# Conv taps in a new order and of another kind, and later transposes of q and k, in a transformer block kernel

## The chip, the cores and the metric

One core of one Trainium2 chip runs the whole kernel. The metric is device time in microseconds (us) for one execution; lower is better. Several runs are made, and their median is given.

## The reference, cut to what matters

The function is one block with two feed-forward parts and a mixer between them, in fp32, for 256 positions and a width of 2048. The change touches the mixer alone, and in it the convolution and the preparation of q and k:

```python
proj = h @ w_in                      # 256 x 2048 times 2048 x 5120
q, k, v, conv_a, conv_g = split(proj)
q = apply_rope(rms_norm(q, q_norm)); k = apply_rope(rms_norm(k, k_norm))   # 16 heads of 64
attn = diff_attention(q, k, v, lam)  # causal softmax of two score maps, their difference times v
u = conv_a * sigmoid(conv_g)         # 1024 channels
u = causal_depthwise_conv(u, conv_w, conv_b)   # 31 taps a channel
u = silu(layer_norm(u))
y = concat(rms_norm(attn), u) @ w_out
```

A depthwise convolution of 31 taps is, per channel, a sum of 31 copies of u, each moved by d = 30 - j positions and multiplied by the channel's weight for tap j.

## The kernel before, in words

Activations stand with the contraction dimension on the partitions, so a weight tile of 512 rows by 512 columns is multiplied in 4 row blocks for 2 position tiles, and each product is made of three matmuls (high times high, high times low, low times high: `mm3`, lines 317 to 319) of an fp32 value split in two fp32r parts. One weight tile is thus 24 matmuls of 512 columns. A weight tile comes by one DMA from SP's queue into `raw`. ScalarE makes the high part of each half of it (`whi`, line 296), VectorE subtracts to get the low part (`wlo`, line 298). `whi` and `wlo` have four buffers each, so four half tiles.

The mixer's projection is a loop over 10 column chunks `ci` of `w_in` (line 1045), each of 4 weight tiles `pc` (3 in the loop for the first three chunks, whose first tiles are done ahead of it). Chunks 0 to 3 are convolution channels, two channel tiles of 128 each (so the convolution's 8 channel tiles are done in two halves of four: half 0 from chunks 0 and 1, half 1 from chunks 2 and 3); chunks 4 to 7 are q, k, q, k (`qk_chunk`, two groups of 4 head pairs), chunks 8 and 9 are v. A chunk's accumulators stay in PSUM until its work is done behind the first tile of the next chunk (`finish_mix`).

Side work is cut into pieces and issued between tiles, in the program's order:

- `later` (lines 159 to 172): functions that are to run n weight tiles later. `tick`, called at the end of every tile's matmuls, counts all entries down and runs from the head of the list while the head's count is at zero or below; an entry behind one that is not due waits for it. The transposes of q and k (line 859) stand here with n = 1, one entry for each of two position tiles; the entry that hands a k group's 8 attention score units to `probs` stands behind them.
- `bg` (lines 147 to 153): convolution taps with a cost in units. `fill(n)` takes from the head until n units are used. `TAPS[ci]` is the n of each tile of chunk ci, `TAPS_OUT` that of the first two tiles of the output projection, after which all is drained and the layer norm of the convolution starts (`conv_ln`).

There are two kinds of tap. A plain tap (`conv_tap`, lines 762 to 773) is one VectorE instruction on one channel tile (multiply and add, line 773), or for j = 30 one ScalarE instruction with the bias (line 771). A wide tap (`conv_wide`, lines 775 to 783) does four channel tiles: four ScalarE multiplies into a block `pr` (line 781) and one VectorE add of 4 x 256 elements (line 783). Before, 8 taps of each half are wide (j = 22 to 29). They are queued when the half's second chunk is done, as one run of 8 at 3 units each, ahead of that chunk's plain taps, behind what is left of the first chunk's.

VectorE's work on a q or k chunk (lines 844 to 855, for each position tile): a scalar step of the root mean square (line 143), which follows ScalarE's eight squares (line 843), then a product with a cosine table (848), two with a sine table (853) and their sum (855). The result `A` comes from `tmp`, a pool of six buffers. After it, four transposes on TensorE (line 830) and copies by ScalarE (833, 835, 836).

The order of instructions on each engine is laid out when the kernel is built, by a list scheduler that follows the program's order and lets an instruction that is ready pass one that waits. On the chip each engine runs its list in that order.

Of the kernel before, what the change touches and what calls it, by code (L numbers as in the profile page):

```python
# [24 lines left out]
P = 128  # L25
D = 2048
S = 256
NT = 2
# [5 lines left out]
DH = 64  # L34
CK = 31
# [12 lines left out]
DUE = ((19, 8), (55, 16), (107, 24), (150, 32))  # L48


TAPS = (6, 5, 6, 6, 6, 6, 8, 6, 6, 6)
TAPS_OUT = 12
WIDE = tuple(range(CK - 9, CK - 1))
RMS_EPS = 1e-6
LN_EPS = 1e-5
LAM_INIT = 0.8 - 0.6 * float(np.exp(-0.3 * 0))
# [20 lines left out]
def block_kernel(ctx: ExitStack, tc: tile.TileContext, x_in, pos_in, w_ada, small, w_gu1, w_dn1,  # L77
# [15 lines left out]
    def nm(s):  # L93
        uid[0] += 1
        return f"{s}_{uid[0]}"

    def blk(shape, dtype=F32):
        return blkp.tile(shape, dtype, tag="blk", name=nm("blk"))

    def tmp(shape, dtype=F32):  # L100
        return tmpp.tile(shape, dtype, tag="tmp", name=nm("tmp"))

    def sm(shape, tag="sm"):
        return smp.tile(shape, F32, tag=tag, name=nm(tag))

    def acc_tile(shape=(P, 512)):
        return accp.tile(list(shape), F32, tag="acc", name=nm("acc"))

    def tp_tile(shape=(P, 512)):
        return tpp.tile(list(shape), F32, tag="tp", name=nm("tp"))  # L110
# [23 lines left out]
    for i in range(4):  # L134
        pc = acc_tile()
# [5 lines left out]
    def rstd_of(ss, n, count, eps):  # L141

        nc.vector.tensor_scalar(out=ss, in0=ss, scalar1=1.0 / count, scalar2=eps, op0=ALU.mult, op1=ALU.add)
        nc.gpsimd.tensor_tensor(out=ss, in0=ss, in1=half[:, :n], op=ALU.pow)


    bg = deque()

    def fill(n):
        while n > 0 and bg:  # L150
            units, fn = bg.popleft()
            fn()
            n -= units
# [7 lines left out]
    def after_tiles(n, fn):  # L161
        later.append([n, fn])
# [44 lines left out]
    def ada_share(r, limit):  # L207
        credit[0] += r
        while credit[0] >= 1.0:
            credit[0] -= 1.0  # L210
            if ada_next[0] < limit:
                ada(ada_next[0])
                ada_next[0] += 1
# [113 lines left out]
    def mm_tile(accs, w, act, k0, start, stop, ts=(0, 1), ks=(0, 4)):  # L327

        for j in range(*ks):
            for t in ts:  # L330
                last_mm[0] = mm3(accs[t], act(k0 + j, t), w(j), start and j == ks[0], stop and j == ks[1] - 1)
        tick()
# [14 lines left out]
    class Norm:  # L347
# [28 lines left out]
        def transposed(self, xn):  # L376
            tp = tp_tile((P, 4, P))
            for j in range(4):
                nc.tensor.transpose(tp[:, j, :], xn[:, j * P:(j + 1) * P], ident)  # L379
            return tp, tmp([P, 4, P])  # L380
# [381 lines left out]
    def conv_tap(cc, i, j):  # L762
        ct = 2 * cc + i
        y = ytile[ct // 4][:, ct % 4, :]
        p0 = _COLS["convw"][0] + ct * CK + j
        w = cst[:, p0:p0 + 1]
        d = CK - 1 - j
        u = uT[cc][:, i, :S - d]
        if d == 0:
            b0 = _COLS["convb"][0] + ct  # L770
            nc.scalar.activation(out=y, in_=u, func=AF.Identity, scale=w, bias=cst[:, b0:b0 + 1])  # L771
        else:
            nc.vector.scalar_tensor_tensor(out=y[:, d:], in0=u, scalar=w, in1=y[:, d:], op0=ALU.mult, op1=ALU.add)  # L773

    def conv_wide(b, j):

        d = CK - 1 - j
        pr = blk([P, 4, S])
        for i in range(4):
            p0 = _COLS["convw"][0] + (4 * b + i) * CK + j  # L780
            nc.scalar.activation(out=pr[:, i, d:], in_=uT[2 * b + i // 2][:, i % 2, :S - d], func=AF.Identity,  # L781
                                 scale=cst[:, p0:p0 + 1])
        nc.vector.tensor_add(out=ytile[b][:, :, d:], in0=pr[:, :, d:], in1=ytile[b][:, :, d:])

    def conv_chunk(cc, accs):
        us = []
        for t in range(NT):
            sg = tmp([P, 256])
            nc.scalar.activation(out=sg, in_=accs[t][:, 256:], func=AF.Sigmoid)
            u = tmp([P, 256])  # L790
            nc.vector.tensor_mul(out=u, in0=accs[t][:, :256], in1=sg)
            us.append(u)

        def rest():
            tp = tp_tile((P, 2, S))
            for t in range(NT):
                for i in range(2):
                    nc.tensor.transpose(tp[:, i, t * P:(t + 1) * P], us[t][:, i * P:(i + 1) * P], ident)
            uT[cc] = blk([P, 2, S])
            nc.scalar.copy(out=uT[cc], in_=tp)  # L800
            if cc % 2:
                for i in range(2):
                    bg.append((0, lambda i=i: conv_tap(cc, i, CK - 1)))
                for j in WIDE:
                    bg.append((3, lambda j=j: conv_wide(cc // 2, j)))
            for j in reversed(range(CK)):
                for i in range(2):
                    if j not in WIDE and not (cc % 2 and j == CK - 1):
                        bg.append((1, lambda i=i, j=j: conv_tap(cc, i, j)))

        after_tiles(1, rest)

# [2 lines left out]
    def qk_chunk(name, g, accs):  # L815
        gc, gs = gcs["qn" if name == "q" else "kn"]
        if name == "q":
            dst = blk([P, 4, S])
            qT[g] = dst
        else:  # L820
            dst = [blk([P, 4, S]) for _ in range(2)]
            nc.gpsimd.memset(dst[0][DH:, :, :], 0.0)
            nc.gpsimd.memset(dst[1][:DH, :, :], 0.0)
            kz[g] = dst

        def transposed(t, A):
            tp = tp_tile((P, 4, P))
            Af = A.rearrange("p h d -> p (h d)")
            for i in range(4):
                nc.tensor.transpose(tp[:, i, :], Af[:, i * P:(i + 1) * P], ident)  # L830
            ts = slice(t * P, (t + 1) * P)
            if name == "q":
                nc.scalar.copy(out=dst[:, :, ts], in_=tp)
            else:
                nc.scalar.copy(out=dst[0][:DH, :, ts], in_=tp[:DH])
                nc.scalar.copy(out=dst[1][DH:, :, ts], in_=tp[DH:])

        for t in range(NT):
            a3 = accs[t].rearrange("p (h d) -> p h d", d=DH)
            sq = tmp([P, 8, DH])  # L840
            rs = sm([P, 8], "rs8")
            for i in range(8):
                nc.scalar.activation(out=sq[:, i, :], in_=a3[:, i, :], func=AF.Square, accum_out=rs[:, i:i + 1])  # L843
            rstd_of(rs, 8, DH, RMS_EPS)
            if name == "q":
                rq_of[g, t] = rs
            A = tmp([P, 8, DH])
            nc.vector.tensor_mul(out=A, in0=a3, in1=gc[:, t, :].unsqueeze(1).to_broadcast([P, 8, DH]))
            B = tmp([P, 8, DH])
            for h2 in range(2):  # L850
                o = slice(32 * h2, 32 * h2 + 32)
                r = slice(32 - 32 * h2, 64 - 32 * h2)
                nc.vector.tensor_mul(out=B[:, :, o], in0=a3[:, :, r],
                                     in1=gs[:, t, o].unsqueeze(1).to_broadcast([P, 8, 32]))
            nc.vector.tensor_add(out=A, in0=A, in1=B)
            if name == "k":
                for i in range(8):
                    nc.scalar.activation(out=A[:, i, :], in_=A[:, i, :], func=AF.Identity, scale=rs[:, i:i + 1])  # L858
            after_tiles(1, lambda t=t, A=A: transposed(t, A))

    def v_chunk(g, accs):
        v = blk([P, NT, 512])
# [182 lines left out]
    for ci in range(10):  # L1045
        p0 = 1 if ci < HOLD else 0
        accs = first[ci][2] if ci < HOLD else [acc_tile() for _ in range(NT)]
        for pc in range(p0, 4):
            if ci == 0 and pc < 3:
                for t in range(NT):  # L1050
                    st.piece(pc + 1, t)
            w = w_tile(w_in[ci, pc], ci == 0 and pc <= PRE)
            if ci == 1 or ci == 0 and pc > 1:
                ada_share(1.0, 104)
            mm_tile(accs, w, act, 4 * pc, pc == 0, pc == 3)
            if pc == p0:
                while pend:
                    finish_mix(*pend.pop(0))
            if pc == 3 and ci < 4:
                conv_chunk(ci, accs)  # L1060
            fill(TAPS[ci])
            for _ in range(UNITS):
                if probs:
                    attn_probs(*probs.popleft())
                if avq:
                    attn_av(*avq.popleft())
        if ci >= 4:
            pend.append((ci, accs))
# [136 lines left out]
```

## Time and profile before

| what | value |
|---|---|
| median of 3 runs | 1851.36 us (1848.5 to 1851.45) |
| the profiled execution's own time | 1849.3 us |
| its span in the profile | 1847.5 us |
| TensorE matmul busy (PE) | 1820.4 us, 99% of the span |
| TensorE weight load busy (PEld) | 1501.3 us, 81% |
| VectorE busy (DVE) | 1436.7 us, 78% |
| ScalarE busy (ACT) | 935.3 us, 51% |
| granted TensorE clock, mean | 0.996 |

Busy shares are means over stages; the projection of the mixer stands at about 770 to 1012 us of the span, its output projection from there to about 1103 us. Instructions overlap at their ends: two that follow each other without a gap start closer together than one lasts, so what an instruction takes of a full engine is read from the distance of starts, and its listed length is a little more.

### The profile page before, as it was taken

The numbers are of one execution on the slowest core, as the hardware profiler recorded it, in microseconds if no ns is written. First come the engines' busy times: TensorE is split into PE (matmuls) and PEld (weight loads), VectorE is DVE, ScalarE is ACT, GpSimd is POOL, SyncE is SP. The second block draws the span as 40 slices with busy tenths as digits, with TensorE's granted clock in tenths as the row PEclk, the third lists the DMA queues.
The fourth block names the chain that finished last, engine by engine and source line by source line (L and its number), as shares of the span: only waits on it lengthen the run. The fifth ranks groups of instructions, "written<-read, shape, count | busy, mean of one in ns | idle before, by whom it ended". The sixth has DMA issues, their size and how long they took to land.

```text
span 1847.5 us, 21913 instructions
## 1 busy us (share of the span) xinstructions
PE 1820.4 (99%) x8247; PEld 1501.3 (81%) x8247; DVE 1436.7 (78%) x1874; ACT 935.3 (51%) x1442; POOL 30.2 (2%) x29
## 2 busy tenths in 40 slices
PE   6999999999999999999999999999999999999999
PEld 5788888888888887888888788888888888888887
DVE  7789969998888777898998768878877765544443
ACT  6554444444444433567798655664444444433332
POOL 0000000000000000000111000000000000000000
PEclk8999999999999999999999999999999999999999
DMA  9888968889889898765444557988777755565552
GB/s 382 348 314 309 337 256 316 336 307 339 322 332 365 335 357 329 283 251 182 171 150 159 177 210 305 334 335 317 274 279 273 275 191 195 183 211 211 199 211 80
DMA packets 72729, 495.91 MB, mean 268 GB/s; under 512 B 8192, under 2 KB 8624, under 8 KB 15152
## 3 DMA queue, kind: packets, MB, share of 16 engines
q1 hardware_dynamic: 72624, 494.53, 72.0%
q8 instruction: 64, 1.05, 0.2%
q14 instruction: 41, 0.34, 0.0%
HBM read 492.37 MB, written 2.12 MB: 268 GB/s over the span
## 4 chain that ended last, share of the span: by engine, by line
PE 90%; DVE 5%; ACT 2%; DMA 2%; issue 1%; POOL 0%; SPq 0%; POOLq 0%; DVEq 0%; ACTq 0%
PE acc L318 29%; PE acc L319 29%; PE acc L317 29%; DVE wlo L298 2%; DVE blk L773 1%; DMA raw<-in_w_ada_dram 1%; PE tp L590 1%; ACT whi L296 1%; PE acc L881 1%; ACT blk L781 1%; PE tp L379 1%; DMA blk<-in_w_ada_dram 1%; DVE raw L183 0%; ACT tmp L858 0%; ACT tmp L843 0%
## 5 line engine op out<-in xcount | busy, mean ns | idle before, releaser
L296 ACT CAST whi<-raw 128x1024 fp32r<-128x1024 f32 (+1 forms) x605 | 628.1, 1047 | 719.6 <-PE acc L319 589.2
L298 DVE TENSOR_TENSOR wlo<-raw,whi 128x1024 fp32r<-128x1024 f32 (+1 forms) x605 | 725.6, 1214 | 318.4 <-ACT whi L296 317.0
L317 PE MATMUL acc<-whi,blk 128*128 128x512 f32 x2448 | 955.7, 393 | 5.8 <-ACT blk L388 2.2
L318 PE MATMUL acc<-wlo,blk 128*128 128x512 f32 x2448 | 956.1, 391 | 3.9 <-DVE wlo L298 3.8
L319 PE MATMUL acc<-whi,blk 128*128 128x512 f32 x2448 | 955.2, 390 | 0.0
L317 PEld LDWEIGHTS acc<-whi,blk 128*128 128x128 f32 x2448 | 460.2, 188 | 102.2 <-ACT whi L296 2.8
L318 PEld LDWEIGHTS acc<-wlo,blk 128*128 128x128 f32 x2448 | 460.4, 188 | 100.9 <-DVE wlo L298 7.6
L319 PEld LDWEIGHTS acc<-whi,blk 128*128 128x128 f32 x2448 | 460.1, 188 | 96.8 <-DVE blk L390 0.9
L183 DVE CUSTOM_DVE_ANT_0 raw<-raw,c_bc 128x2048 f32<-128x2048 f32 x142 | 324.5, 2287 | 7.1 <-DMA raw<-in_w_ada_dram 7.0
L470 ACT COPY blk<-acc 128x512 f32<-128x512 f32 x88 | 50.0, 590 | 60.0 <-PE acc L319 58.0
L773 DVE SCALAR_TENSOR_TENSOR blk<-blk,cst,blk 128x245 f32<-128x245 f32 (+21 forms) x176 | 70.8, 468 | 0.6 <-ACT blk L771 0.5
L582 DVE TENSOR_TENSOR blk<-acc,blk 128x512 f32<-128x512 f32 x88 | 57.0, 684 | 0.3
L319 PE MATMUL acc<-blk,blk 128*128 128x512 f32 x112 | 43.7, 392 | 0.0
L317 PE MATMUL acc<-blk,blk 128*128 128x512 f32 x112 | 43.7, 393 | 0.0
L318 PE MATMUL acc<-blk,blk 128*128 128x512 f32 x112 | 43.7, 390 | 0.0
L298 DVE TENSOR_TENSOR blk<-raw,blk 128x1024 fp32r<-128x1024 f32 x28 | 33.8, 1222 | 1.6 <-ACT blk L296 1.6
L584 DVE TENSOR_TENSOR blk<-blk 128x256 f32<-128x256 f32 x88 | 33.5, 420 | 0.7 <-ACT blk L583 0.7
L583 ACT ACTIVATE blk<-blk 128x256 f32<-128x256 f32 x88 | 32.3, 412 | 1.2 <-DVE blk L582 1.1
L296 ACT CAST blk<-raw 128x1024 fp32r<-128x1024 f32 x28 | 28.8, 1050 | 7.0 <-DMA raw<-in_w_dn_dram 5.9
L336 DVE TENSOR_TENSOR blk<-tp,blk 128x512 fp32r<-128x512 f32 x44 | 30.0, 685 | 2.2 <-ACT blk L335 2.2
L345 ACT ACTIVATE tmp<-xall 128x512 f32<-128x512 f32 x22 | 13.8, 632 | 30.3 <-DVE xall L643 17.0
L590 PEld LDWEIGHTS tp<-cst,blk 128*128 128x128 f32 x176 | 21.6, 140 | 6.6 <-DVE blk L336 1.4
(151 smaller groups left out, 717.3 us busy)
## 6 DMA issues: line engine op xcount, KB each, us to landing
raw<-in_w_gu_dram SPq DMA_DIRECT2D x161, 1024.0 KB, 5.4
raw<-in_w_ada_dram SPq DMA_DIRECT2D x142, 1024.0 KB, 6.1
raw<-in_w_dn_dram SPq DMA_DIRECT2D x88, 1024.0 KB, 4.8
raw<-in_w_in_dram SPq DMA_DIRECT2D x40, 1024.0 KB, 4.8
raw<-in_w_out_dram SPq DMA_DIRECT2D x16, 1024.0 KB, 4.8
raw<-in_w_gu_dram SPq DMA_DIRECT2D x8, 768.0 KB, 5.4
blk<-in_w_gu_dram SPq DMA_DIRECT2D x10, 512.0 KB, 13.9
blk<-gate_line SPq DMA_DIRECT2D x6, 512.0 KB, 6.3
```

The costliest lines, as they stand in the source:

```text
L183: nc.vector.tensor_tensor_reduce(out=raw, in0=raw, in1=c_bc, scale=1.0, scalar=0.0, op0=ALU.mult, op1=ALU.add, accum_out=ada_cols[g][:, j ...
L296: nc.scalar.copy(out=hi[:, :m, :], in_=rw)
L298: nc.vector.tensor_sub(out=lo[:, :m, :], in0=rw, in1=hi[:, :m, :].bitcast(F32))
L317: nc.tensor.matmul(acc, ah, wh, start=start, stop=False)
L318: nc.tensor.matmul(acc, ah, wl, start=False, stop=False)
L319: return nc.tensor.matmul(acc, al, wh, start=False, stop=stop)
L470: last_part[0] = nc.scalar.copy(out=parts[c][:, t, :], in_=accs[t])
L582: nc.vector.tensor_add(out=p[:, t, :], in0=accs[t], in1=p[:, t, :])
L583: nc.scalar.activation(out=p[:, t, :256], in_=p[:, t, :256], func=AF.Silu)
L584: nc.vector.tensor_mul(out=p[:, t, 256:], in0=p[:, t, :256], in1=p[:, t, 256:])
L590: nc.tensor.transpose(tp[:, i, t * P:(t + 1) * P], p[:, t, 256 + i * P:256 + (i + 1) * P], ident)
L773: nc.vector.scalar_tensor_tensor(out=y[:, d:], in0=u, scalar=w, in1=y[:, d:], op0=ALU.mult, op1=ALU.add)
```

## The change

The wide taps of half 0 become twelve (j = 18 to 29), those of half 1 stay eight. In the second chunk of a half they no longer come as one run: the plain taps are queued in order, and a wide tap is put in behind every third of them, at 2.6 units. The two ScalarE taps (j = 30) of that chunk cost a unit each as in the first. `TAPS` gets two numbers for each chunk: one for its first tile in the loop, behind which the previous q, k or v chunk is finished, and one for the others. The transposes of q and k go into `later` with n = 2, and `A` is a slice of one block for both position tiles, from the pool of 28 blocks in place of `tmp`.

```diff
-TAPS = (6, 5, 6, 6, 6, 6, 8, 6, 6, 6)
+TAPS = ((6, 6), (5, 5), (6, 6), (6, 7), (7, 7), (2, 7), (2, 7), (2, 7), (2, 7), (4, 7))
 TAPS_OUT = 12
-WIDE = tuple(range(CK - 9, CK - 1))
+
+WIDE = (tuple(range(CK - 13, CK - 1)), tuple(range(CK - 9, CK - 1)))
@@ conv_chunk
-            if cc % 2:
-                for i in range(2):
-                    bg.append((0, lambda i=i: conv_tap(cc, i, CK - 1)))
-                for j in WIDE:
-                    bg.append((3, lambda j=j: conv_wide(cc // 2, j)))
-            for j in reversed(range(CK)):
-                for i in range(2):
-                    if j not in WIDE and not (cc % 2 and j == CK - 1):
-                        bg.append((1, lambda i=i, j=j: conv_tap(cc, i, j)))
+            wide = WIDE[cc // 2]
+            plain = [(i, j) for j in reversed(range(CK)) for i in range(2) if j not in wide]
+            for n, (i, j) in enumerate(plain):
+                bg.append((1, lambda i=i, j=j: conv_tap(cc, i, j)))
+                if cc % 2 and n % 3 == 1 and n // 3 < len(wide):
+                    bg.append((2.6, lambda j=wide[n // 3]: conv_wide(cc // 2, j)))
@@ qk_chunk
+        both = blk([P, NT, 8, DH])
...
-            A = tmp([P, 8, DH])
+            A = both[:, t]
...
-            after_tiles(1, lambda t=t, A=A: transposed(t, A))
+            after_tiles(2, lambda t=t, A=A: transposed(t, A))
@@ the loop over chunks
-            fill(TAPS[ci])
+            fill(TAPS[ci][pc > p0])
```

## Rows read from the trace of the kernel before

**Rows 1.** The page's head and its part 1: busy time of each engine.

```profile
span 1847.5 us, 21913 instructions
PE 1820.4 (99%) x8247; PEld 1501.3 (81%) x8247; DVE 1436.7 (78%) x1874; ACT 935.3 (51%) x1442; POOL 30.2 (2%) x29
```

**Rows 2.** Windows: length, busy PE, PEld, DVE, ACT, POOL; clock; DMA share; GB/s.

```profile
838.00:854.00 16.00, 16.00 (x73) 13.22 (x72) 13.32 (x13) 12.41 (x25) 0.00 (x0) 1.00 0.59 216
854.00:876.00 22.00, 22.00 (x100) 18.21 (x99) 16.52 (x24) 15.67 (x31) 0.00 (x0) 1.00 0.38 136
876.00:898.00 22.00, 20.18 (x92) 16.30 (x91) 22.00 (x43) 13.01 (x42) 5.18 (x4) 1.00 0.54 192
954.00:985.00 31.00, 30.75 (x167) 25.98 (x166) 27.17 (x55) 30.12 (x106) 3.27 (x2) 1.00 0.41 150
```

**Rows 3.** Timeline of TensorE: start, length, line, operation, count, idle time before it.

```profile
875.55 0.39 PE L318 MATMUL acc<-wlo,blk 128*128 128x512 f32 x1
...
876.00 0.61 PE L317 MATMUL acc<-whi,blk 128*128 128x512 f32 x2
876.63 0.49 PE L318 MATMUL acc<-wlo,blk 128*128 128x512 f32 x1
...
882.21 1.04 PE L830 MATMUL tp<-cst,tmp 128*128 128x128 f32 x8
885.05 0.50 PE L318 MATMUL acc<-wlo,blk 128*128 128x512 f32 x1 [1.81 <-DVE wlo L298]
...
944.77 0.48 PE L317 MATMUL acc<-whi,blk 128*128 128x512 f32 x1
945.44 0.50 PE L318 MATMUL acc<-wlo,blk 128*128 128x512 f32 x1 [0.19 <-DVE wlo L298]
...
968.46 0.40 PE L317 MATMUL acc<-whi,blk 128*128 128x512 f32 x1
969.10 0.46 PE L881 MATMUL acc<-blk,blk 128*128 128x128 f32 x2 [0.25 <-ACT blk L835]
...
1014.02 1.05 PE L920 MATMUL acc<-blk,blk 128*128 128x128 f32 x7 [0.74 <-ACT blk L864]
```

**Rows 4.** Groups by line, 838 to 1056 us: count; busy, mean ns; idle before.

```profile
L298 DVE TENSOR_TENSOR wlo<-raw,whi 128x1024 fp32r<-128x1024 f32 x67 | 80.9, 1226 | 10.5 <-ACT whi L296 10.4
L296 ACT CAST whi<-raw 128x1024 fp32r<-128x1024 f32 x66 | 69.6, 1064 | 34.0 <-PE acc L319 28.9 <-issue 3.3 <-DVE wlo L298 1.7
...
L781 ACT ACTIVATE blk<-blk,cst 128x248 f32<-128x248 f32 (+7 forms) x64 | 26.7, 500 | 0.0
L783 DVE TENSOR_TENSOR blk<-blk,blk 128x992 f32<-128x992 f32 (+7 forms) x16 | 19.3, 1208 | 2.7 <-ACT blk L781 2.6
```

**Rows 5.** Timeline of VectorE about the first q chunk.

```profile
862.55 1.21 DVE L783 TENSOR_TENSOR blk<-blk,blk 128x1008 f32<-128x1008 f32 x1 [0.85 <-ACT blk L781]
...
877.62 0.17 DVE L143 TENSOR_SCALAR rs<-rs 128x8 f32<-128x8 f32 x1
...
882.25 1.61 DVE L773 SCALAR_TENSOR_TENSOR blk<-blk,cst,blk 128x240 f32<-128x240 f32 x4
883.76 2.37 DVE L298 TENSOR_TENSOR wlo<-raw,whi 128x1024 fp32r<-128x1024 f32 x2
886.03 2.35 DVE L773 SCALAR_TENSOR_TENSOR blk<-blk,cst,blk 128x238 f32<-128x238 f32 x6
```

**Rows 6.** Timeline of ScalarE, where the last four wide taps of half 0 run.

```profile
860.82 6.48 ACT L781 ACTIVATE blk<-blk,cst 128x252 f32<-128x252 f32 x16
867.21 2.94 ACT L296 CAST whi<-raw 128x1024 fp32r<-128x1024 f32 x3
```

**Rows 7.** Timeline of VectorE between the two position tiles of the first k chunk.

```profile
904.65 1.22 DVE L298 TENSOR_TENSOR wlo<-raw,whi 128x1024 fp32r<-128x1024 f32 x1
```

**Rows 8.** Timeline of VectorE: the last plain tap, and the layer norm's first sum.

```profile
1022.08 0.45 DVE L773 SCALAR_TENSOR_TENSOR blk<-blk,cst,blk 128x226 f32<-128x226 f32 x1
...
1030.81 1.22 DVE L955 TENSOR_TENSOR blk<-blk,blk 128x1024 f32<-128x1024 f32 x1
```

## The prediction

> **What bounds the kernel now.** I read the page's part 1 first: TensorE is busy for 1820.4 of 1847.5 us, so 27 us are the most that any change of order can give in the whole kernel [rows 1]. Most of those lie at the start, where this change does nothing. What matters is TensorE's idle time in the mixer, and for that I went through its timeline from 772 to 1070 us and compared the distance of starts with the undisturbed one: two matmuls of 512 columns between 875.55 and 876.00 make 0.225 us each, so a weight tile of 24 is 5.4 us. Five places stand out [rows 3]. At 876.00 two matmuls take 0.63 where 0.45 is normal: 0.18 lost. At 885.05 the engine sat idle for 1.81, until the subtract of line 298 was done. At 944.77 the next start is 0.67 away: 0.44 lost, to the same line. At 968.46 it is 0.64: 0.41 lost, to the copies of the transposed k. At 1014.02 the idle time is 0.74, before the first product with v. Together 3.6 us, or 0.19% of the time. All but the last two are a VectorE that comes late with the low part of a weight tile.
>
> Why it is late is in the windows. From 838 to 854 and from 854 to 876 us VectorE is busy for 13.32 of 16 and 16.52 of 22 us, so it idles for 8.2 us; from 876 to 898 it is busy for all of 22 [rows 2]. In the first of these stretches ScalarE is given a run of wide taps: 16 multiplies without a break from 860.82 to 867.21, with the casts for the next weights queued behind them at 867.21 [rows 6]. VectorE has then nothing to subtract from and nothing but wide adds, which wait for ScalarE (0.85 at 862.55). It enters the first q chunk at 877.62 without a lead, does the chunk and six plain taps, and comes to the next tile's subtract at 883.76 [rows 5].
>
> **The prices.** On a full VectorE four plain taps take 883.76 - 882.25 = 1.51, so 0.38 each; two subtracts take 886.03 - 883.76 = 2.27, so 1.135 each, for a listed length of 1.226 [rows 4, 5]. The add of a wide tap is listed at 1.208, with the same overlap 1.12. A ScalarE multiply takes 6.39 / 16 = 0.40 [rows 6], a wide tap 1.6 there.
>
> **Part 1: twelve wide taps in half 0.** Four taps of four channel tiles leave the plain ones: 16 x 0.38 = 6.1 us go from VectorE, 4 x 1.12 = 4.5 come back, and ScalarE gets 16 x 0.40 = 6.4. Cover: ScalarE has 16 - 12.41 and 22 - 15.67, together 9.9 us of idle time in the two stretches where half 0 runs [rows 2]. If that cover is gone, 6.4 is what it costs. I take nothing for it.
>
> [...]
>
> **Part 2: the new order and the new TAPS.** I counted what each tile's fill takes, from both lists. VectorE's load moves as follows. Chunks 3 and 4: from 25 plain and 8 wide (18.5 us) to 35 and 11 (25.6), so +7.1, against 8.2 us of idle time there. Chunks 5 to 7: from 76 and 1 (30.0) to 58 and 4 (26.5), so -3.5, in the stretch where VectorE is full. Chunk 8: from 3 and 7 to 15 and 5, +2.3. Chunk 9: 24 to 21 plain, -1.1. The output projection: 17 plain taps to none, -6.5. In each chunk's first tile the fill falls from 6 or 8 units to 2, so at the first q chunk four taps leave the way to the subtract.
>
> *The first q chunk.* With VectorE entering it at 877.62 as now, the subtract starts at 882.25 in place of 883.76, and the matmul of 885.05 could start at 883.54. TensorE is done with the tile at 882.21, and with part 3 it has no transposes to do there: it waits for 1.33 and does the eight transposes (1.04) a tile later, 2.37 in all, where 885.05 - 882.21 = 2.84 pass now. That is a gain of 0.5. If the scheduler puts the subtract between the two position tiles, as it does in the first k chunk [rows 7], the whole idle time of 1.81 goes. On the other side the +7.1 could eat the lead so that VectorE enters the chunk later: up to the 0.85 that one wide add waits, and the gain turns into -0.4. Bounds -0.4 and 1.8. The nearest row is that of the k chunk, the same code one chunk on, but it had other taps about it, so I take 1.3.
>
> *The other subtracts.* Of the 0.18 at 876.00 I take 0.1 (0 to 0.18), of the 0.44 at 944.77 I take 0.3 (-0.3 to 0.44), since the second q chunk loses four taps of its first tile but gets two attention units there (part 3).
>
> *The tail.* The layer norm's first sum stands at 1030.81, 8.7 us behind the last tap at 1022.08 [rows 8], behind subtracts of its own tile: earlier taps bring it nothing. What VectorE no longer does at 1010 to 1022 lets the small steps of the attention's norm come sooner, and ScalarE reach the copies of v: of the 0.74 at 1014.02 I take 0.3 (0 to 0.5).
>
> **Part 3: transposes two tiles behind.** No instruction is added: 32 transposes and their copies move back by one tile, with the entry that hands out the score units behind them, so that group 0's 8 units run in chunk 6's tiles 2 and 3 and chunk 7's first, not in tiles 1 to 3. No DMA moves and SP's queue is not touched; POOL's power steps stay where they are. The wait for the copies of k at 968.46 stays, as the scores still follow their transposes in the same tile: 0 (-0.2 to 0.4). In chunk 7 the entries for q stand ahead of two score units' transposes, so that four transposed blocks come due in one tick with two PSUM buffers: the third waits for a copy by ScalarE, at most two casts' length, 2 x 1.06 [rows 4]; I take a cost of 0.2 (0 to 1.0, as other matmuls can pass). `A` in a block of the large pool frees two small buffers and takes one of 28; the trace shows no wait for either, so nothing.
>
> **Sum.** 1.3 + 0.1 + 0.3 + 0.3 - 0.2 = 1.8 us gained. From the profiled execution's 1849.3 that is 1847.5. The median of the runs is 2.1 above that execution, so against the median it is 1849.6.
>
> **Rivals.** *A, the wide adds wait at the head of VectorE's queue.* Now 16 of them wait for 2.7 us, 0.17 each, with a worst of 0.85 [rows 4, 5]. In the new order each has plain taps ahead but also a subtract behind it, and the cast it depends on waits for TensorE. The lead that four weight buffers allow is three half tiles less a cast and a subtract, 8.1 - 1.06 - 1.23 = 5.8 us. In chunks 3 and 4 the slack is 8.2 - 7.1 + 5.8 = 6.9, or 0.63 for each of 11 wide adds; in chunks 7 and 8, where there is no idle time, each wait counts. From 8 x (w - 0.17) = 1.8 on, so w = 0.4 us a wide add, the change is slower; at w = 0.75 it costs 1.4 + 4.6 - 1.8 = 4.2, which gives 1855.6. For it: the single wait of 0.85. Against: that one came in a run of wide taps, which is what goes. [...]
>
> *B, all of the stalls go.* VectorE with its load evened out keeps its lead everywhere: 0.18 + 1.81 + 0.44 + 0.41 + 0.74 = 3.6, which gives 1847.8. For it: chunks 5 to 7 are relieved by 3.5 us where VectorE is full. Against: the waits at 968.46 and 1014.02 are for ScalarE copies that no tap stands before.
>
> *C, nothing comes of it.* The q chunk itself (877.62 to 882.25, of which two taps are 0.8) is what holds up the subtract, and its lead is spent by the +7.1: gain 0, 1851.4.
>
> *D, ScalarE becomes the bound.* [...] From 954 to 985 us ScalarE is busy for 30.12 of 31 [rows 2]. If the 6.4 us of new multiplies fell on a full engine, 6.4 - 1.8 = 4.6 would be lost, 1856.0. Against: they fall at 838 to 876, and chunk 8 loses two wide taps.
>
> **How the numbers follow.** A measurement of this kernel tells 0.2%, or 3.7 us, from no change. Forecast 0.58 (faster 0.08, same 0.49, slower 0.01), B 0.17 (faster 0.10, same 0.07), C 0.11 (same 0.10, slower 0.01), A 0.10 (same 0.03, slower 0.07), D 0.04 (same 0.01, slower 0.03). So faster 0.18, same 0.70, slower 0.12. The range goes from B's 1847.8, less 1.8 that the runs differ among themselves, to the lower half of A, 1853.4.
>
> **What would show it.** The step on the run of wide taps: in the new trace VectorE is busy for over 20 of the 22 us before the first q chunk. The step on the first q chunk: the idle time before the tile's first low-part matmul is under 1.3. The step on the tail: no tap behind chunk 9, and the layer norm's first sum no earlier than one us relative to its tile. Rival A would show as waits of line 783 over 8 us in sum. The prediction is wrong if the idle time of TensorE in the mixer grows, or if it falls by more than the 3.6 that I found.

## The result: slower, by two stops of TensorE

The changed kernel takes 1857.53 us (median of 8 runs, 1856.45 to 1860.01), the kernel before 1851.47 in as many runs beside it: a ratio of 1.0035, with a 95% interval of 1.0026 to 1.0044. That is 6.5 us slower (0.0035 x 1851; the two medians as they stand differ by 6.1), where 1.8 us faster was forecast, and outside the range. The profiled execution took 1856.71 us, 7.4 more than the one of before. Of these 7.4, 1.2 lie ahead of the mixer, where the program is unchanged (the traces of the experiments stand -0.3 to 3.1 us from the one of before there). So times of the two traces are compared with 1.2 us taken off: the first matmul behind chunk 4 starts at 877.20, before at 876.00 [rows 3].

The page's head and its part 1, of the kernel after:

```profile
span 1854.9 us, 21921 instructions
PE 1823.9 (98%) x8247; PEld 1502.1 (81%) x8247; DVE 1434.0 (77%) x1862; ACT 942.1 (51%) x1458; POOL 27.1 (1%) x29
```

Against [rows 1] VectorE has 2.7 us less to do and ScalarE 6.8 more: 16 plain taps less and 4 wide adds more on the one, 16 multiplies more on the other, as counted. TensorE has the same 8247 matmuls and yet 3.5 us more of busy time. The windows show where matmuls take longer, and which clock was granted there. Windows of the kernel after (columns as in [rows 2]; the first two are the first two of [rows 2], moved by 1.2 us):

```profile
839.20:855.20 16.00, 16.00 (x73) 13.21 (x72) 14.77 (x21) 13.83 (x29) 0.00 (x0) 1.00 0.44 161
855.20:877.20 22.00, 22.00 (x101) 18.20 (x99) 20.88 (x31) 18.62 (x39) 0.00 (x0) 1.00 0.51 185
...
876.00:898.00 22.00, 19.28 (x80) 15.32 (x79) 22.00 (x37) 13.78 (x48) 5.19 (x4) 0.92 0.47 174
...
888.00:891.50 3.50, 3.50 (x10) 2.76 (x9) 3.50 (x5) 1.05 (x1) 0.00 (x0) 0.53 0.54 185
...
954.00:985.00 31.00, 27.85 (x126) 22.17 (x127) 27.36 (x45) 29.24 (x91) 3.27 (x2) 0.94 0.31 115
...
964.00:970.00 6.00, 2.90 (x12) 1.56 (x10) 6.00 (x12) 6.00 (x29) 1.64 (x1) 0.98 0.00 0
970.00:973.20 3.20, 3.20 (x9) 2.33 (x10) 3.10 (x6) 3.20 (x10) 0.00 (x0) 0.50 0.26 54
```

Up to 877 us TensorE misses nothing. From 876 to 898 it now does 80 instructions where it did 92, and from 954 to 985 it does 126 where it did 167 [rows 2]. In each of the two stretches it stops for some microseconds, and behind the stop the granted clock is 0.53 and 0.50 for about 3 us, where the windows up to 877 us have 1.00. Its timeline at the two stops and at the tail (kernel after; columns as in [rows 3]):

```profile
877.20 0.39 PE L318 MATMUL acc<-whi,blk 128*128 128x512 f32 x1
...
882.64 0.61 PE L318 MATMUL acc<-whi,blk 128*128 128x512 f32 x2
883.85 0.63 PE L828 MATMUL tp<-cst,blk 128*128 128x128 f32 x4 [0.60 <-DVE blk L854]
886.60 0.50 PE L319 MATMUL acc<-wlo,blk 128*128 128x512 f32 x1 [2.12 <-DVE wlo L299]
...
888.32 0.63 PE L320 MATMUL acc<-whi,blk 128*128 128x512 f32 x1
888.75 0.63 PE L318 MATMUL acc<-whi,blk 128*128 128x512 f32 x1
...
891.29 0.39 PE L318 MATMUL acc<-whi,blk 128*128 128x512 f32 x1
...
964.80 0.61 PE L318 MATMUL acc<-whi,blk 128*128 128x512 f32 x2
967.15 1.74 PE L828 MATMUL tp<-cst,blk 128*128 128x128 f32 x4 [1.73 <-ACT blk L857]
969.83 0.95 PE L828 MATMUL tp<-cst,blk 128*128 128x128 f32 x2 [0.94 <-ACT blk L857]
970.43 0.77 PE L319 MATMUL acc<-wlo,blk 128*128 128x512 f32 x1
...
973.40 0.39 PE L318 MATMUL acc<-whi,blk 128*128 128x512 f32 x1
...
1021.46 0.60 PE L934 MATMUL tp<-cst,tmp 128*128 128x128 f32 x4
1022.11 2.94 PE L919 MATMUL acc<-blk,blk 128*128 128x128 f32 x24
```

How to read the first stop: from 882.64 to 891.29 are 8.65 us. In them are 15 matmuls of 512 columns at 0.227 and four transposes at 0.13, together 3.9, so about 4.7 are lost. Of these 0.60 and 2.12 are shown as idle, and the rest is mostly the clock: from 888.32 to 888.75, in the window at 0.53, is one matmul, 0.43 in place of 0.227, and there are 8 such. The second stop is in the second k chunk: from 964.80 to 973.40 are 8.6 us with 9 matmuls and 6 transposes (2.8), so 5.8 are lost. At the tail the first products with v start at 1022.11 with no idle time before them, where [rows 3] had 0.74.

Summed in this way over 800 to 1035 us (start distances above the undisturbed one), TensorE loses 11.2 us, before 4.4: at the first q chunk 4.6 against 1.9, at the second k chunk 5.8 against 0.4, everywhere else 0.7 against 2.1. The difference of 6.8, with the 1.2 ahead of the mixer and less some 0.7 that TensorE makes up behind it, accounts for the 7.4 between the two executions.

Why the engines that feed it are late. The group that answers to the last of [rows 4], kernel after:

```profile
L784 DVE TENSOR_TENSOR blk<-blk,blk 128x992 f32<-128x992 f32 (+11 forms) x20 | 23.9, 1197 | 4.3 <-ACT blk L782 3.7
```

VectorE's timeline, kernel after, at a wide add, the first q chunk, the second k chunk, the last plain taps and the layer norm's first sum (it answers to [rows 5] and [rows 8]):

```profile
863.74 1.20 DVE L784 TENSOR_TENSOR blk<-blk,blk 128x996 f32<-128x996 f32 x1 [0.81 <-ACT blk L782]
...
880.20 0.16 DVE L144 TENSOR_SCALAR rs<-rs 128x8 f32<-128x8 f32 x1
...
880.87 1.20 DVE L784 TENSOR_TENSOR blk<-blk,blk 128x1016 f32<-128x1016 f32 x1
...
885.33 1.21 DVE L299 TENSOR_TENSOR wlo<-raw,whi 128x1024 fp32r<-128x1024 f32 x1
...
956.79 1.19 DVE L784 TENSOR_TENSOR blk<-blk,blk 128x992 f32<-128x992 f32 x1 [2.02 <-ACT blk L782]
...
967.29 1.20 DVE L784 TENSOR_TENSOR blk<-blk,blk 128x1004 f32<-128x1004 f32 x1
...
969.00 2.35 DVE L299 TENSOR_TENSOR wlo<-raw,whi 128x1024 fp32r<-128x1024 f32 x2
...
1012.18 1.18 DVE L774 SCALAR_TENSOR_TENSOR blk<-blk,cst,blk 128x227 f32<-128x227 f32 x3
...
1038.91 1.22 DVE L954 TENSOR_TENSOR blk<-blk,blk 128x1024 f32<-128x1024 f32 x1
```

It enters the q chunk at 880.20, where it was 877.62 [rows 5] (1.2 of the 2.6 us are the shift of the whole trace), and reaches the subtract at 885.33, with a wide add in the middle of the chunk; it idles for no more than 0.4 us between 864 and 888. And ScalarE's timeline, kernel after (it answers to [rows 6]):

```profile
862.02 6.45 ACT L782 ACTIVATE blk<-blk,cst 128x249 f32<-128x249 f32 x16
...
873.46 2.93 ACT L297 CAST whi<-raw 128x1024 fp32r<-128x1024 f32 x3
...
961.39 1.07 ACT L297 CAST whi<-raw 128x1024 fp32r<-128x1024 f32 x1
...
966.43 2.08 ACT L857 ACTIVATE blk<-blk,rs 128x64 f32<-128x64 f32 x8
...
969.18 2.02 ACT L857 ACTIVATE blk<-blk,rs 128x64 f32<-128x64 f32 x8
```

The run of 16 wide multiplies before the q chunk is still one run. A plain tap has no ScalarE part, so taps that alternate on VectorE still come to ScalarE one wide tap behind the other. Behind it, the third of the casts from 873.46 on, at 875.35, is the one whose subtract starts at 885.33.

### The profile page after: what moved, and what is told of

It reads as the page before. It is cut to its first block, busy times and chain, and to the rows that moved or that the text cites. A ratio compares the mean times of both kernels' runs of the same rounds, so it can differ in the third digit from the quotient of the medians.

```text
span 1854.9 us, 21921 instructions
## 1 busy us (share of the span) xinstructions
PE 1823.9 (98%) x8247; PEld 1502.1 (81%) x8247; DVE 1434.0 (77%) x1862; ACT 942.1 (51%) x1458; POOL 27.1 (1%) x29
## 3 DMA queue, kind: packets, MB, share of 16 engines
HBM read 492.37 MB, written 2.12 MB: 267 GB/s over the span
## 4 chain that ended last, share of the span: by engine, by line
PE 92%; DVE 3%; ACT 2%; DMA 1%; issue 1%; POOL 0%; SPq 0%; POOLq 0%; DVEq 0%; ACTq 0%
PE acc L319 30%; PE acc L320 30%; PE acc L318 30%; PE tp L591 1%; DVE wlo L299 1%; DMA blk<-in_w_gu_dram 1%; PE acc L880 1%; PE tp L380 1%; DMA blk<-in_w_ada_dram 1%; DVE blk L774 0%; ACT blk L782 0%; ACT whi L297 0%; DVE blk L784 0%; PE acc L919 0%; ACT tmp L842 0%
## 5 line engine op out<-in xcount | busy, mean ns | idle before, releaser
L774 DVE SCALAR_TENSOR_TENSOR blk<-blk,cst,blk 128x241 f32<-128x241 f32 (+21 forms) x160 | 64.8, 461 | 0.8 <-ACT blk L772 0.5
L782 ACT ACTIVATE blk<-blk,cst 128x248 f32<-128x248 f32 (+11 forms) x80 | 33.3, 500 | 0.0
```

## The experiments

Each experiment ran in five rounds, beside the kernel before on the same chip. The column of lost time is the sum above, of each kernel's one profiled execution: at the first q chunk, at the second k chunk, elsewhere.

| kernel | median, before beside it (us) | ratio [95%] | TensorE loses (us) |
|---|---|---|---|
| before | | | 1.9 + 0.4 + 2.1 |
| after | 1857.53, 1851.47 | 1.0035 [1.0026, 1.0044] | 4.6 + 5.8 + 0.7 |
| e1_n1 | 1852.77, 1850.95 | 1.0010 [1.0001, 1.0019] | 4.9 + 1.2 + 0.8 |
| e2_x_only | 1855.90, 1850.95 | 1.0028 [1.0017, 1.0038] | 1.9 + 5.8 + 1.0 |
| e3_old_taps | 1853.52, 1850.95 | 1.0012 [1.0004, 1.0021] | 4.4 + 0.7 + 1.4 |
| e4_wide8 | 1850.86, 1850.95 | 0.9998 [0.9989, 1.0007] | 2.3 + 0.9 + 0.6 |
| e5_order_only | 1852.32, 1850.85 | 1.0006 [0.9997, 1.0015] | 5.9 + 0.2 + 0.4 |
| e6_wide8_n1 | 1851.15, 1850.85 | 1.0001 [0.9992, 1.0010] | 3.8 + 0 + 2.2 |
| e7_cast_first | 1850.59, 1850.85 | 0.9997 [0.9988, 1.0006] | 0 + 0 + 3.6 |
| e8_warm | 1854.09, 1850.85 | 1.0016 [1.0007, 1.0025] | 0.4 + 1.7 + 0.7, and 5.4 added |
| f1_before_cast | 1851.47, 1849.99 | 1.0006 [0.9998, 1.0015] | 0 + 0 + 4.3 |
| f2_wide8_n1_cast | 1847.91, 1849.99 | 0.9990 [0.9981, 0.9999] | 0 + 0 + 2.7 |
| f3_n1_cast | 1849.45, 1849.99 | 0.9996 [0.9988, 1.0005] | 0.2 + 0 + 1.6 |
| f4_x_cast | 1850.56, 1849.99 | 0.9999 [0.9990, 1.0008] | 0 + 0 + 3.4 |

The sum of the last column follows the ratio within some 2 us. e6 and f3 stand furthest off: their profiled executions were 2.2 us above and 1.4 below their medians.

**e1_n1**, the change with the transposes one tile behind:

```diff
-            after_tiles(2, lambda t=t, A=A: transposed(t, A))
+            after_tiles(1, lambda t=t, A=A: transposed(t, A))
```

> The changed kernel with the transposes of q and k one weight tile behind again (the block for A stays). Load theory: what costs the time is VectorE and ScalarE work that the new order and the new TAPS put in front of the first q chunk and the second k chunk; so the two stops of TensorE (2.7 us about the first q chunk, some 4 us about the second k chunk) stay, and the ratio to the kernel before stays at 1.003 to 1.004. Rival, transposes: the list puts the transposes at places where TensorE then waits for them; with one tile the old places come back, and the ratio falls to 1.001 or less.

The stop at the second k chunk went, the one at the first q chunk stayed with its fall of the clock (0.57 from 888 to 892 us), and 2.5 per mille of the 3.5 were gone. The load theory's time was a miss, and the time is the rival's (1.001). So the new taps make the first stop, whatever the transposes do.

**e2_x_only**, the transposes alone: the kernel before with `both` and n = 2.

```diff
+        both = blk([P, NT, 8, DH])
...
-            A = tmp([P, 8, DH])
+            A = both[:, t]
...
-            after_tiles(1, lambda t=t, A=A: transposed(t, A))
+            after_tiles(2, lambda t=t, A=A: transposed(t, A))
```

> The kernel before with the transposes two tiles behind and A in a block, nothing else. Load theory: same as before, ratio 0.999 to 1.001. Rival, transposes: slower by some 3 to 5 us, ratio 1.002 to 1.003, with waits of TensorE for line 854 to 858's results.

The edit that I had put down at 0.2 us costs 2.8 per mille by itself, 5.2 us: the rival's size, but not the wait that it named. The first stop is as before. The second is new; TensorE's timeline in e2_x_only:

```profile
967.56 1.04 PE L830 MATMUL tp<-cst,blk 128*128 128x128 f32 x8
971.60 0.73 PE L317 MATMUL acc<-whi,blk 128*128 128x512 f32 x2 [3.00 <-ACT whi L296]
```

and ScalarE's:

```profile
957.78 1.10 ACT L296 CAST whi<-raw 128x1024 fp32r<-128x1024 f32 x1
...
966.90 3.71 ACT L781 ACTIVATE blk<-blk,cst 128x250 f32<-128x250 f32 x9
970.46 2.03 ACT L296 CAST whi<-raw 128x1024 fp32r<-128x1024 f32 x2
```

Not one cast is done between 957.78 and 970.46: the chunk's squares and scalings and sixteen wide multiplies stand ahead of it, the last nine as one run. In the kernel before, the same stretch has casts at 957.39, 960.70, 963.56 (two) and 967.38. The matmuls of the next tile had no weights. No transpose is involved; the edit changed where the casts stand in ScalarE's list.

**e3_old_taps**, the change with the numbers of `TAPS` as before (each for both places):

```diff
-TAPS = ((6, 6), (5, 5), (6, 6), (6, 7), (7, 7), (2, 7), (2, 7), (2, 7), (2, 7), (4, 7))
+TAPS = ((6, 6), (5, 5), (6, 6), (6, 6), (6, 6), (6, 6), (8, 8), (6, 6), (6, 6), (6, 6))
```

> The changed kernel with the old number of units in each tile (6, 5, 6, 6, 6, 6, 8, 6, 6, 6 for both tiles of a pair). Load theory: chunk 4 gets 24 units in place of 28 and the first tiles get their taps back; the stop about the first q chunk shrinks to about that of before (2 us), without a fall of the clock, ratio 1.000 to 1.002. Rival, transposes: unchanged, 1.003 to 1.004.

The first stop stays (1.60 and 1.16 idle, then a granted clock of 0.57 from 888 to 892 us), the second goes although the transposes are two tiles behind. The time is within the load theory's range, but not by its way, since the first stop is what stays. So with twelve wide taps neither n = 2 (this run) nor the new `TAPS` (e1_n1) makes the second stop alone; the two together do.

**e4_wide8**, the change with 8 wide taps in both halves:

```diff
-WIDE = (tuple(range(CK - 13, CK - 1)), tuple(range(CK - 9, CK - 1)))
+WIDE = (tuple(range(CK - 9, CK - 1)), tuple(range(CK - 9, CK - 1)))
```

> The changed kernel with eight wide taps in both halves. Load theory: 4 x 1.6 us of ScalarE work go from the stretch before the first q chunk, so the stop there becomes shorter than 2 us and the ratio falls by 0.001 to 0.0015, to 1.002 to 1.0025; the stop at the second k chunk stays. Rival, transposes: unchanged, 1.003 to 1.004.

All of the loss is gone, with n = 2 in place, which is more than either theory allowed: the second stop went too. VectorE's entry into the first q chunk and the last two matmuls of TensorE's tile, in e4_wide8:

```profile
879.18 0.17 DVE L144 TENSOR_SCALAR rs<-rs 128x8 f32<-128x8 f32 x1
...
882.69 0.61 PE L318 MATMUL acc<-whi,blk 128*128 128x512 f32 x2
```

VectorE enters 4.0 us ahead of the end of the tile (two matmuls of 0.227 behind 882.69, so 883.14); in the change this lead is 883.09 - 880.20 = 2.9, before 882.21 - 877.62 = 4.6. TensorE's idle time there is the same 2.12, but in one piece and without a fall of the clock (1.00 from 886 to 892 us).

**e5_order_only**, the alternation by itself: e4_wide8 with the old `TAPS`, n = 1 and `A` from `tmp`.

> The kernel before with the new order of the taps alone: eight wide in both halves, one behind every third plain tap, the old units in each tile, transposes one tile behind, A in a small buffer. Load theory (too much side work ahead of the first q chunk): TensorE's stop there is no longer than the 2 us of before, ratio 0.999 to 1.000. Rival, order (the alternation itself puts casts and subtracts late, since VectorE's adds wait for ScalarE between them): a stop of over 3 us about the first q chunk, ratio 1.001 to 1.002.

At the edge of what can be told, to the slower side: neither theory's time, and a stop near the rival's. Idle time of 2.17 and 0.71 at the first q chunk (a wide add stands between its two position tiles), and eleven matmuls at a lower clock (0.50 from 890 to 894 us).

**e6_wide8_n1**, e4_wide8 with n = 1.

> The changed kernel with eight wide taps in both halves and the transposes one tile behind. If the wide taps of half 0 cost some 3.5 per mille and the transposes some 2.5 each by itself, the two gains add up: 0.997 to 0.998. If there is one stop at each of two places, which either undo keeps under the length at which the clock falls, it is no better than with eight wide taps alone: 0.999 to 1.000.

No difference to the kernel before or to e4_wide8, in time the second of the two cases: with 8 wide taps the transposes cost nothing. Its stop is as long as that of e4_wide8, and there the clock fell. TensorE's timeline at the stop, in e4_wide8:

```profile
885.97 0.50 PE L319 MATMUL acc<-wlo,blk 128*128 128x512 f32 x1 [2.12 <-DVE wlo L299]
```

the window behind it:

```profile
886.00:889.00 3.00, 3.00 (x13) 2.46 (x14) 3.00 (x6) 0.79 (x2) 1.21 (x2) 1.00 0.15 30
```

TensorE's timeline at the stop in e6_wide8_n1:

```profile
886.69 0.50 PE L319 MATMUL acc<-wlo,blk 128*128 128x512 f32 x1 [2.12 <-DVE wlo L299]
```

and a window behind that, with the clock at 0.50:

```profile
888.00:891.00 3.00, 3.00 (x8) 2.31 (x7) 3.00 (x9) 0.52 (x1) 0.00 (x0) 0.50 0.46 145
```

**e7_cast_first**, the change with the same instructions, but each weight tile's load, casts and subtracts put earlier in the lists from chunk 4 on:

```diff
-            w = w_tile(w_in[ci, pc], ci == 0 and pc <= PRE)
+            with tc.high_priority(offset=SOONER) if ci > 3 else nullcontext():
+                w = w_tile(w_in[ci, pc], ci == 0 and pc <= PRE)
```

> The changed kernel with the loads, casts and subtracts of the weight tiles of chunks 4 to 9 listed ahead of other work (a higher priority for the list scheduler); the same instructions. List theory: the stops are there because casts and subtracts stand behind side work on ScalarE and VectorE, so both shrink below 1 us, the clock does not fall, and the ratio is 0.998 to 1.000. Rival, load: the engines have too much to do in these stretches in any order; the stops move but their sum stays, ratio 1.002 to 1.004.

Both stops and the falls of the clock are gone. Windows of e7_cast_first over the two places:

```profile
882.00:888.00 6.00, 6.00 (x28) 4.95 (x28) 6.00 (x11) 5.81 (x22) 0.42 (x1) 1.00 0.61 216
964.00:970.00 6.00, 6.00 (x29) 4.93 (x28) 6.00 (x11) 6.00 (x25) 1.64 (x1) 1.00 0.69 246
```

VectorE and ScalarE are as full as in the change, and TensorE misses nothing. I counted casts and subtracts off against each other: between 870 and 890 us a subtract starts 1.2 to 1.8 us behind the start of its cast here; in the change it is 2.2 to 10.0, in the kernel before 3.8 to 10.3. So at the late subtracts the weights had been cast, and the subtracts stood in line. One such pair in e7_cast_first:

```profile
881.68 1.03 ACT L297 CAST whi<-raw 128x1024 fp32r<-128x1024 f32 x1
...
882.94 1.21 DVE L299 TENSOR_TENSOR wlo<-raw,whi 128x1024 fp32r<-128x1024 f32 x1
```

What is left in one place is 2.4 us at 980 to 984, where the softmax's exponentials now stand behind casts.

**e8_warm**, the change with twelve matmuls of 512 columns more at the head of the second tile of chunks 5 and 8, into a PSUM buffer that nobody reads (5.4 us of work that the function does not need):

```diff
-        nc.tensor.matmul(acc, ah, wh, start=start, stop=False)
+        m0 = nc.tensor.matmul(acc, ah, wh, start=start, stop=False)
+        if warm[0]:
+            n, warm[0] = warm[0], 0
+            spare = tp_tile()
+            with tc.issue_after(m0.ins):
+                for _ in range(n):
+                    m0 = nc.tensor.matmul(spare, ah, wh, start=True, stop=True)
...
+            if (ci, pc) in ((5, 1), (8, 1)):
+                warm[0] = 12
```

> The changed kernel with twelve more matmuls of 512 columns (12 x 0.227 = 2.7 us, results not used) on TensorE at the head of the second tile of chunk 5 and of chunk 8, where it stops. Clock theory: what follows each stop runs at half speed for some 8 and 6 matmuls because TensorE stood still; with work in the stops it stays at full clock, and although 5.4 us of work are added the time falls by up to 1.6 + 1.2 us: ratio 1.0015 to 1.003. Rival: the slow matmuls are slow for another reason, operands coming late or a shared port; they stay slow, and the added work that does not fit into the stops makes it 1.004 or more.

TensorE's timeline at the first stop, in e8_warm:

```profile
883.10 2.88 PE L326 MATMUL tp<-whi,blk 128*128 128x512 f32 x12
...
886.86 0.50 PE L327 MATMUL acc<-wlo,blk 128*128 128x512 f32 x1 [0.21 <-DVE wlo L299]
```

and the windows behind both stops:

```profile
888.00:892.00 4.00, 4.00 (x20) 3.27 (x18) 4.00 (x5) 1.06 (x1) 0.15 (x1) 1.00 0.59 188
970.00:974.00 4.00, 4.00 (x19) 3.31 (x18) 3.90 (x7) 3.95 (x7) 0.00 (x0) 1.00 0.73 250
```

With more work the kernel is 1.9 per mille (1.0035 less 1.0016), 3.5 us, faster than the change, and the intervals do not touch. The added matmuls lie in time in which TensorE waited, the clock stays at 1.00, and the subtract comes no sooner. In the traces, what is lost and what is added come to 0.4 + 1.7 + 5.4 = 7.5 us at the two stops, where the change loses 4.6 + 5.8 = 10.4: 2.9 us less. So by the traces (2.9) and by the runs (3.5) about half of the 6.5 was the clock, and the rest the wait itself.

**f1_before_cast, f2_wide8_n1_cast, f3_n1_cast, f4_x_cast**: the edit of e7_cast_first in the kernel before, in e6_wide8_n1, in e1_n1 and in e2_x_only.

> The kernel before with the loads, casts and subtracts of chunks 4 to 9 listed ahead, nothing else. List theory: the stop of 2.0 us at the first q chunk and the 0.4 at the second go, the rest stays: ratio 0.998 to 0.999. Rival, load: VectorE is full from 876 to 970 us, so what is put ahead there only makes other work late; ratio 0.9995 to 1.001.

> The new order and the new units, eight wide taps in both halves, transposes one tile behind, and the casts ahead. List theory: no stop of over 1 us is left in chunks 4 to 9, ratio 0.9975 to 0.999. If the new order is worth anything beyond the stop at the first q chunk, this is faster than the kernel before with the casts ahead; if not, they are the same within 0.001.

> The changed kernel with the transposes one tile behind and the casts ahead. List theory: the one stop that this kernel had without the casts ahead (at the first q chunk, 3.3 us and a fall of the clock) goes: 0.998 to 0.9995. Rival, load: twelve wide taps are too much for ScalarE and VectorE ahead of the first q chunk: 1.000 to 1.001.

> The kernel before with the transposes two tiles behind, A in a block, and the casts ahead. List theory: what the later transposes cost (2.8 per mille) came from the casts that fell behind a run of nine wide multiplies at the second k chunk; with the casts ahead it is gone, 0.998 to 1.0005. Rival, transposes: the score units that come a tile later are what costs; 1.002 to 1.003 stays.

f4 settles the transposes: with the casts and subtracts early, their 2.8 per mille are gone. f2 (1847.91 us) is faster than both kernels, though its interval leaves out 1.0000 only just; that of f3 does not, so whether the alternation is worth anything by itself is not shown. f1 was a miss: in the kernel before both stops go, and one of the same size comes, since two casts now stand ahead of the exponentials. TensorE in f1_before_cast:

```profile
986.17 0.71 PE L881 MATMUL acc<-blk,blk 128*128 128x128 f32 x4 [1.83 <-ACT tmp L892]
```

and the window behind it:

```profile
987.00:990.20 3.20, 3.20 (x11) 2.65 (x11) 2.56 (x12) 3.02 (x11) 0.00 (x0) 0.50 0.75 246
```

So "feeders first" is not a gain by itself. It takes the loss out of this change; the waits that it leaves in the traces (f1, f4, e7 at 980 to 986 us) are in the main those for the exponentials.

## Why the prediction was wrong, step by step

**The first q chunk: forecast 1.3 gained (bounds -0.4 and 1.8), measured 2.7 lost.** This step failed. I took VectorE's entry "at 877.62 as now", with up to 0.85 of delay as the far end. It entered 1.4 later (2.6 less the shift of 1.2), since the 7.1 us of new load in chunks 3 and 4 did not all find room in the 8.2 us of idle time. From 839.2 to 877.2 us VectorE is busy for 14.77 + 20.88 = 35.65, in the same two stretches before for 13.32 + 16.52 = 29.84 [rows 2], so 5.8 of the 7.1 found room and 1.3 were pushed behind them. The idle time that is left (1.2 in the first stretch, 1.1 in the second) lies where VectorE waits for a cast or for a wide tap's multiplies, as at 863.74; its list put no other tap there. With 8 wide taps (e4_wide8) the lead is 4.0 in place of 2.9, so 1.1 of the 1.7 by which the lead fell are the four wide taps. Nor was the subtract freed of its taps: `TAPS` asks for 2 units in the first tile, but two plain taps and a wide add stood between the entry and the subtract, 5.1 us in all against 6.1 before and 4.6 forecast (882.25 - 877.62). Of the 3.1 us by which 885.33 misses 882.25, 1.2 are the shift, 1.4 the entry and 0.5 the tap work. The idle time before the first low-part matmul, forecast under 1.3, is 2.12. Of the 2.7 lost, 1.1 are longer waits, and 1.6 are the clock, for which the sum had no term.

The reason that I gave for the old stop was wrong as well. I read the run of ScalarE's wide multiplies as holding up the casts. The cast of the late subtract had started at 873.48, ten microseconds before the subtract at 883.76 [rows 5]; VectorE's list held it up. ScalarE, kernel before:

```profile
873.48 1.06 ACT L296 CAST whi<-raw 128x1024 fp32r<-128x1024 f32 x1 [1.66 <-PE acc L319]
```

Nor does the trace of before show a subtract that the add at 862.55 held back: the next one starts at 868.47, and its cast only at 867.21 [rows 6]. Only e2_x_only has the stop that I described, and at another place.

**The transposes: forecast 0.2 lost (0 to 1.0), measured 5.4 at the second k chunk.** This step failed too. I followed the moved instructions, and the cost was in those that were not moved. The wait that the 0.2 stood for, in chunk 7, is at most 0.2, at 953.60; the loss is elsewhere. The edit gave the builder of the lists another order of due work, and in e2_x_only it put the cast behind nine wide multiplies. In the change the cast of 961.39 was in time, but its subtract, by the same count, is that of 969.00, 7.6 us later, behind two wide adds and the k chunk's own steps. Six of the eight transposes even stand earlier in TensorE's list than before: two matmuls into the second tile behind their chunk (at 967.15 and 969.83), where before they followed that whole tile. There they wait for the scaling of line 857. e3, e4 and e7 each keep n = 2 and have 0.9 or less there. Why the builder placed them so is not in the trace and stays open.

**The clock: no term in the sum.** Behind both stops TensorE ran at 0.53 and 0.50 for about 3 us, 1.6 us for eight matmuls at the first and 1.0 to 1.3 at the second; e8_warm took it away and, with 5.4 us of work more, was 3.5 us faster. The stop of 1.81 in [rows 3] had no such fall behind it (1.00 from 885 to 890 us), and I read no further.

**What held.** The small terms: 0.18 at 876, 0.44 at 945 and 0.74 at 1014 us were forecast to give 0.7 and gave about 1.3 of their 1.4. No plain tap stands behind chunk 9; the last are at 1012.18, and the layer norm's first sum, at 1038.91, has moved by 8.1, by which TensorE is late there too. The step "VectorE is busy for over 20 of the 22 us" came true with 20.88, and was the sign of the harm, not of the gain. The cover of ScalarE held too: its 4.4 us more in the two stretches before the q chunk (13.83 + 18.62 against 12.41 + 15.67) cost nothing there by themselves.

**The rivals.** D came nearest in time (1856.0), A next (1855.6). Of A the first half held: what slack chunks 3 and 4 had was too little. Its sign was not there: the wide adds wait for 3.7 us in place of over 8. Of these 2.02 are one wait, at 956.79, 5 us before VectorE enters the second k chunk (at 961.76); yet it enters that chunk 3.5 us before the end of TensorE's tile, 3.9 before, so little of the loss comes from it. In the main the wide adds do harm by standing in line, not by waiting. D expected ScalarE full at 954 to 985 us; it is busy for 29.24 of 31 there, less than before, and though it is full in the 6 us of the stop, so it is in e7_cast_first, which loses nothing there. That run has the same wide taps as the change and costs nothing (0.9997). B and C had the wrong sign or none.

The parts do not add up: transposes alone 2.8, taps alone 1.0 (e1_n1), both 3.5 per mille; with 8 wide taps, none. What each of them moves is where casts and subtracts stand among the side work.

## What to carry to other kernels

Before side work is put into an engine's idle time, count how long the instructions that feed the busiest engine already stand in line there (here casts of ten microseconds' age) and put those first; idle time in which the engine waits for another engine's result (2.3 us here) is no reserve. A change of when something falls due can change the lists of all engines, so read the new lists around every place where feeders and side work meet, not only where the moved instructions stand. Price a stop of TensorE at more than its idle time, since the clock may fall behind it (2.12 us of idle time cost 3.8 in e6_wide8_n1, where it fell to 0.50, and 2.3 in e4_wide8, where it stayed at 1.00).

## What the runs showed of the hardware

The same stop may or may not cost the clock. Idle times of 2.12 us at the same place left it at 1.00 in e4_wide8 and took it to 0.50 in e6_wide8_n1; 1.81 left it at 1.00 in the kernel before, and 1.83 in f1_before_cast took it to 0.50. So idle time alone does not tell which stop brings the fall; what does, no run here shows. The first stops of the change (0.53), e1 (0.57), e3 (0.57) and e5 (0.50) and the second of the change (0.50) and e2 (0.63 from 972 to 976 us) brought the fall; a wait of 1.59 in f4_x_cast (at 982.52) did not (1.00 from 980 to 988 us). Each of these is one execution; whether another one of the same kernel loses the clock at the same stop is not shown. Twelve useless matmuls in each of two such stops left the clock at 1.00 behind them (888 to 892 and 970 to 974 us in e8_warm) and made the kernel 3.5 us faster.
